# A chunked recurrent scan: key products and their uses in the off-diagonal quarters of the tensor array

## The chip, the cores and the metric

The kernel runs on one core of one Trainium2 chip. The metric is the device time of one execution in microseconds (us). Three runs of the kernel before took 4102.95, 4102.1 and 4114.9 us; the median is 4102.95 us.

## The reference

A two-layer encoder trunk works on two batches, 256 and 1024 tokens of 1024 features, that is 16 heads of 64. Layer 0 mixes tokens with a bidirectional RWKV-7 recurrence, layer 1 with neighbourhood attention, and an MLP follows each. The change is in the recurrence, which is this for every head and direction:

```
def step(S, inp):
    r_t, w_t, k_t, v_t, a_t, b_t = inp
    sa = jnp.einsum('bhvk,bhk->bhv', S, a_t)
    S = S * w_t[:, :, None, :] + sa[..., None] * b_t[:, :, None, :] + v_t[..., None] * k_t[:, :, None, :]
    return S, jnp.einsum('bhvk,bhk->bhv', S, r_t)
```

S is a 64 x 64 state. The backward direction runs the same from the other end, and the two results are added.

## The kernel before, in words

**The stage.** Projections and preparations come first and write to DRAM, per head pair m and direction d, the scaled streams `ar` (columns 0:64 from a, 64:128 from r) and `bk` (columns 0:64 from b, 64:128 from k). Then `scan` (L732) does the recurrence, and the gate, the MLPs and the attention follow. Only `scan` and what it calls is changed.

**Chunks and jobs.** Tokens are taken in chunks of L = 64. Two heads lie on the 128 partitions, head e of the pair on partitions 64e to 64e+63. A job is 16 chunks of one head pair (`scan_job`, L779), in 4 groups g of 4 chunks, for both directions. There are 10 jobs, one after the other, of 16 time steps each; in a step, one chunk of each direction goes through the recurrence. Everything else prepares later steps or finishes earlier ones.

**One pair of matmuls.** `pair` (L967) issues two 64 x 64 matmuls, head 0 on the rows and columns 0 to 63 of the array and head 1 on rows and columns 64 to 127. These are the two diagonal quarters of the array. Operands are fp32.

**Preparation, per group and direction** (so once in two steps): `prod` (L804) makes `aps` = b·(a, r) for 4 chunks, a mask on VectorE turns it into `zb` (L813), `store` sends a part through DRAM for a triangular inverse that VectorE works out in 31 updates per job (`rank1`, L846: a product into `tmp`, L851, and an addition into `q`, L853; "update pair" below), and `merge1` and `merge2` (L895, L903) finish the inverse Q on TensorE (`yps`, `qps`), with copies on ScalarE. `kprod` (L917) makes `kps` = k·(a, r), `kmask` (L924) masks it into `zk` on VectorE, and `ktr` (L928) transposes b and k into `lps`, which ScalarE copies to `lt` (L937). aps, yps, kps, qps and lps, and the transposes `zps` of finished results, share two PSUM buffers in turn (pool `pa`, tag "aps").

**One step of one direction** (`scan_step`, L972), each row a pair of matmuls:

- s0: w = zk(a part)·v. s1: w += a·S, then ScalarE copies w to `up` (L988).
- s1b: yo = zk(r part)·v, yo += r·S; sn = S, sn += k·v.
- s2: us = Q·up, copied to `u` (L1005). s3: sn += b·u, scaled to the next state S (L1011).
- s4: yo += zb·u; VectorE copies or adds yo into y (L1018, L1020).

So a chain w → up → us → u → sn → S → w runs through TensorE and ScalarE for each direction. Each direction has three PSUM banks: `wu` for w and us, `sn`, and `yo`.

**What sets the order.** `at(t, f)` files a piece of work under a time in steps; all pieces are sorted by it and every engine issues its instructions in that order (L765 to L768). An engine that waits at one instruction holds all behind it. Loads go through SyncE's queue (SP) in the same way.

## Time and profile before

| what | value |
| --- | --- |
| median of three runs | 4102.95 us |
| profiled execution, device time | 4111.2 us |
| its span, first to last instruction | 4109.4 us |
| mean granted TensorE clock | 0.969 of full speed |
| TensorE busy in the span | 95% |
| VectorE, ScalarE, GpSimd busy | 56%, 38%, 33% |

In the profile, PE is TensorE's matmuls and PEld its weight loads, DVE is VectorE, ACT is ScalarE, POOL is GpSimd. An fp32 matmul leaves two PE records, one for each of its two passes, so that a pair of matmuls shows as x4. A PE record's duration holds the way through the array, on which the next matmuls already run; what a pair costs is the distance from its start to the start of the next one. "Idle before" is time in which the engine sat idle, with what ended it.

### The profile page before, as it was taken

Reading aid. Unit: us, or ns where it says so; the run is one execution under the profiler, and the core shown is the slowest. Engines: PE = TensorE matmul, PEld = TensorE weight load, DVE = VectorE, ACT = ScalarE, POOL = GpSimd, SP = SyncE. Lnnn points to the kernel's source line nnn. Section 1 sums busy time; section 2 is a strip of 40 time slices with the busy share of each in tenths; the row PEclk is TensorE's granted clock in tenths of the full one; section 3 lists DMA queues with packets and bytes.
Section 4 is the critical chain, followed back from the end, with each engine's and each line's share of the span. In section 5 each row is a group of like instructions: output and inputs, shape, how many; then the busy total and the mean of one; then the engine's idle time right before and its main releaser. Section 6 shows DMA issues by size and latency. Waiting matters only on the chain.

```text
span 4109.4 us, 91128 instructions
## 1 busy us (share of the span) xinstructions
PE 3914.9 (95%) x36820; PEld 3338.7 (81%) x36820; DVE 2290.3 (56%) x4861; ACT 1565.4 (38%) x3788; POOL 1337.8 (33%) x1252
## 2 busy tenths in 40 slices
PE   8989888999999899999999998999989999999999
PEld 5765577898989787888888888887778888888888
DVE  6777743656556457555555563255563755555555
ACT  6776641455555442111111123366563211111111
POOL 4446541112122334222222242244442422222222
PEclk9987888999999999999999999999999999999999
DMA  4226564665554241111111115354455101101101
GB/s 141 71 101 221 207 204 123 154 152 142 135 139 106 82 159 47 42 42 37 36 42 37 36 45 169 101 122 97 111 141 181 46 32 42 42 32 42 42 31 62
DMA packets 429893, 389.65 MB, mean 95 GB/s; under 512 B 246464, under 2 KB 331840, under 8 KB 429472
## 3 DMA queue, kind: packets, MB, share of 16 engines
q1 hardware_dynamic: 395056, 322.48, 27.6%
q10 hardware_dynamic: 34416, 61.35, 4.2%
q8 instruction: 289, 4.73, 0.5%
q14 instruction: 132, 1.08, 0.1%
HBM read 265.26 MB, written 124.44 MB: 95 GB/s over the span
## 4 chain that ended last, share of the span: by engine, by line
PE 80%; DVE 6%; ACT 4%; DMA 4%; issue 2%; POOL 2%; SPq 1%; ACTq 0%; DVEq 0%; POOLq 0%
PE ps L95 18%; PE ps L96 18%; PE ps L97 18%; PE yo L970 2%; PE sn L970 2%; PE wu L970 2%; PE vps L510 2%; PE kps L970 2%; PE lps L970 2%; PE vps L511 1%; PE vps L512 1%; PE aps L970 1%; PE op L1810 1%; DVE q L853 1%; PE pt L1753 1%
## 5 line engine op out<-in xcount | busy, mean ns | idle before, releaser
L1356 DVE TENSOR_TENSOR x<-ps,x 128x256 f32<-128x256 f32 x1488 | 815.2, 596 | 644.9 <-PE ps L97 644.6
L95 PE MATMUL ps<-ah,whi 128*128 128x512 f32 (+1 forms) x2304 | 843.5, 366 | 0.0
L96 PE MATMUL ps<-al,whi 128*128 128x512 f32 (+1 forms) x2304 | 825.7, 358 | 0.4 <-POOL al L1246 0.4
L97 PE MATMUL ps<-ah,wlo 128*128 128x512 f32 (+1 forms) x2304 | 822.6, 357 | 1.8 <-DVE wlo L90 1.5
L90 POOL TENSOR_TENSOR wlo<-raw,whi 128x1024 fp32r<-128x1024 f32 (+1 forms) x178 | 390.3, 2193 | 850.1 <-ACT whi L89 824.3
L95 PE MATMUL ps<-hh,whi 128*128 128x512 f32 (+1 forms) x1536 | 547.9, 357 | 9.5 <-DVE x L1356 9.5
L96 PE MATMUL ps<-hl,whi 128*128 128x512 f32 (+1 forms) x1536 | 546.6, 356 | 0.0
L97 PE MATMUL ps<-hh,wlo 128*128 128x512 f32 (+1 forms) x1536 | 545.9, 355 | 0.0
L95 PEld LDWEIGHTS ps<-ah,whi 128*128 128x128 f32 x2304 | 434.4, 189 | 72.2 <-issue 8.0
L97 PEld LDWEIGHTS ps<-ah,wlo 128*128 128x128 f32 x2304 | 433.4, 188 | 73.0 <-DVE wlo L90 1.9
L96 PEld LDWEIGHTS ps<-al,whi 128*128 128x128 f32 x2304 | 434.6, 189 | 62.8 <-issue 1.0
L89 ACT CAST whi<-raw 128x1024 fp32r<-128x1024 f32 (+1 forms) x206 | 200.4, 973 | 709.4 <-PE ps L96 630.1
L1335 POOL TENSOR_TENSOR rl<-rl 128x512 f32<-128x512 f32 (+1 forms) x192 | 174.0, 906 | 505.9 <-PE ps L97 462.4
L95 PEld LDWEIGHTS ps<-hh,whi 128*128 128x128 f32 x1536 | 291.5, 190 | 54.0 <-DVE x L1356 11.4
L97 PEld LDWEIGHTS ps<-hh,wlo 128*128 128x128 f32 x1536 | 291.7, 190 | 41.8
L96 PEld LDWEIGHTS ps<-hl,whi 128*128 128x128 f32 x1536 | 291.6, 190 | 40.6
L1334 ACT ACTIVATE rl<-ps 128x512 f32<-128x512 f32 (+1 forms) x192 | 100.8, 525 | 555.8 <-PE ps L97 555.8
L1337 ACT CAST hh<-rl 128x512 fp32r<-128x512 f32 (+1 forms) x192 | 105.5, 550 | 323.8 <-POOL rl L1335 323.8
L1338 DVE TENSOR_TENSOR hl<-rl,hh 128x512 fp32r<-128x512 f32 (+1 forms) x192 | 119.8, 624 | 143.2 <-ACT hh L1337 142.6
L1747 POOL TENSOR_TENSOR s<-s,mx 128x384 f32<-128x384 f32 (+1 forms) x150 | 109.8, 745 | 163.4 <-DVE mx L1746 113.6
L1052 POOL TENSOR_TENSOR y<-y,mu 128x512 f32<-128x512 f32 x18 | 20.3, 1125 | 404.6 <-DVE mu L1049 404.6
L1011 ACT ACTIVATE S<-sn,dall 128x64 f32<-128x64 f32 x288 | 90.9, 316 | 156.8 <-PE sn L970 155.0
(301 smaller groups left out, 8262.8 us busy)
## 6 DMA issues: line engine op xcount, KB each, us to landing
raw<-in_w_down_dram SPq DMA_DIRECT2D x64, 512.0 KB
raw<-in_w_up_dram SPq DMA_DIRECT2D x64, 512.0 KB
ar<-ar_d SPq DMA_DIRECT2D x80, 256.0 KB
bk<-bk_d SPq DMA_DIRECT2D x80, 256.0 KB
ar_d<-ar ACTq DMA_DIRECT2D x32, 512.0 KB
bk_d<-bk ACTq DMA_DIRECT2D x32, 512.0 KB
bs<-tab SPq DMA_DIRECT2D x128, 96.0 KB
v_d<-vt ACTq DMA_DIRECT2D x80, 128.0 KB
```

Source lines behind the costliest of these rows:

```text
L89: nc.scalar.copy(hi[:, cs], raw)
L90: lo_eng.tensor_tensor(out=lo[:, cs], in0=raw, in1=hi[:, cs].bitcast(F32), op=ALU.subtract)
L95: mm(ps, sh, mh, start=first, stop=False)
L96: mm(ps, sh, ml, start=False, stop=False)
L97: mm(ps, sl, mh, start=False, stop=last)
L970: self.nc.tensor.matmul(out, w, x, start=kw.get("start", True), stop=kw.get("stop", True))
L1334: nc.scalar.activation(r[:, :n], ps[:, :n], AF.Relu)
L1335: nc.gpsimd.tensor_tensor(out=r[:, :n], in0=r[:, :n], in1=r[:, :n], op=ALU.mult)
L1337: nc.scalar.copy(hh[:, :n], r[:, :n])
L1338: nc.vector.tensor_tensor(out=hl[:, :n], in0=r[:, :n], in1=hh[:, :n].bitcast(F32), op=ALU.subtract)
L1356: nc.vector.tensor_tensor(out=xv, in0=ps[:, :n], in1=xv, op=ALU.add)
L1747: nc.gpsimd.tensor_tensor(out=s[:, :nk], in0=s[:, :nk], in1=mx[:, 2:3].to_broadcast([P, nk]), op=ALU.mult)
```

## The change

`kprod` writes head e's product to the other half of its PSUM tile, partitions of head 1 - e. Its matmul then uses the array's rows of head e and columns of head 1 - e, an off-diagonal quarter. `zk` so has the heads' halves swapped. Its uses, w = zk·v in s0 and yo = zk·v in s1b, read the swapped half and a second copy of v whose halves are swapped too, and write the plain half: these are off-diagonal as well. v is loaded twice for it, into a tile with two planes.

The banks are dealt anew: w has one alone, us lies beside sn in `su`, yo stays. us then starts without clearing its bank, except at the end of a sequence, where no sn precedes it.

The filed times move: s0 from t - 0.22 to t - 0.66, s1b from t + 0.06 to t + 0.01, s4 from t + 0.70 to t + 0.67, and r·S moves from s1b to s4, behind zb·u. The four parts of kprod move from t + 0.80 and on to t - 0.02 and on, so that each stands behind one of the four parts of prod; kmask moves from t + 1.25 to t + 0.60, right behind the mask of aps; kload from t - 1.9 to t - 2.8. bk has 4 buffers instead of 3, zk 5 instead of 3.

```
-        grow(self.r_v, fx, "v", [P, 16, L], 2)
+        grow(self.r_v, fx, "v", [P, 2, 16, L], 2)
...
-  for x, n in (("wu", P), ("sn", L), ("yo", L))] for d in range(2)]
+  for x, n in (("w", L), ("su", P), ("yo", L))] for d in range(2)]
...
-                self.pair(lambda e, z: (ps[z, c, :], bk[z, c, 64:128], ar[z, c, :]))
+                self.pair(lambda e, z: (ps[self.half(1 - e), c, :], bk[z, c, 64:128], ar[z, c, :]))
...
-            at(t - 1.9, kload)
-            at(t + 1.25, kmask)
+            at(t - 2.8, kload)
+            at(t + 0.60, kmask)
             for c in range(4):
-                at(t + c * 0.11 + 0.80, lambda c=c, f=kprod: f(c))
+                at(t + c * 0.133 - 0.02, lambda c=c, f=kprod: f(c))
...
-                for e in range(2):
-                    nc.sync.dma_start(vt[64 * e:64 * e + 64, k:k + n], ...)
+                for i in range(2):
+                    for e in range(2):
+                        nc.sync.dma_start(vt[self.half(e ^ i), i, k:k + n], ...)
...
+    def half(self, e):
+        return slice(64 * e, 64 * e + 64)
...
         def s0():
-            self.pair(lambda e, z: (w()[z], zk[z, c, 0:64], vt[z, cc, :]), stop=new)
+            self.pair(lambda e, z: (w()[z], zk[half(1 - e), c, 0:64], vt[half(1 - e), 1, cc, :]), stop=new)
...
         def s1b():
-            self.pair(lambda e, z: (yo()[z], zk[z, c, 64:128], vt[z, cc, :]), stop=False)
-            if S is not None:
-                self.pair(lambda e, z: (yo()[z], ar[z, c, 64:128], S[z]), start=False, stop=False)
+            self.pair(lambda e, z: (yo()[z], zk[half(1 - e), c, 64:128], vt[half(1 - e), 1, cc, :]), stop=False)
...
         def s2():
-            self.pair(lambda e, z: (us()[z], Q[z, cc, d, :], up[z]))
+            self.pair(lambda e, z: (us()[z], Q[z, cc, d, :], up[z]), start=end, skip=True)
...
         def s4():
-            self.pair(lambda e, z: (yo()[z], zb[z, c, 64:128], u[z]), start=False)
+            self.pair(lambda e, z: (yo()[z], zb[z, c, 64:128], u[z]), start=False, stop=S is None)
+            if S is not None:
+                self.pair(lambda e, z: (yo()[z], ar[z, c, 64:128], S[z]), start=False)
...
-        at(t - 0.22, s0)
+        at(t - 0.66, s0)
         at(t, s1)
-        at(t + 0.06, s1b)
+        at(t + 0.01, s1b)
         at(t + 0.33, s2)
...
-        at(t + 0.70, s4)
+        at(t + 0.67, s4)
```

The order of instructions shows it in two places. The first is on TensorE, where the last transposes of a group (`lps`) end and the next group's aps begins, in the third job; the numbers of the names are buffers, 7206 and 7208 belong to direction 0, 7209 and 7211 to direction 1. Before:

```order
L970 MATMUL lps<-cst,bk 64x64 x4
L970 MATMUL aps<-ar_7174,bb_6166 64x128 [waits DMAHW4_49,DMAHW2_49,PE_49]
L970 MATMUL aps<-ar_7174,bb_6166 64x128
L970 MATMUL wu_7206<-S,ar_7176 64x64 [waits Activation_49]
L970 MATMUL wu_7206<-S,ar_7176 64x64
L970 MATMUL yo_7208<-v_7168,zk 64x64 [waits DVE_49]
L970 MATMUL yo_7208<-v_7168,zk 64x64
L970 MATMUL yo_7208<-S,ar_7176 64x64 x2
```

And now:

```order
L974 MATMUL lps<-cst,bk 64x64 x4
L974 MATMUL aps<-ar_7174,bb_6166 64x128 [waits DMAHW7_49,DMAHW5_49,PE_49]
L974 MATMUL aps<-ar_7174,bb_6166 64x128
L974 MATMUL kps<-ar_7179,bk 64x128 [waits Activation_49]
L974 MATMUL kps<-ar_7179,bk 64x128
L974 MATMUL w_7206<-S,ar_7176 64x64 [waits Activation_49]
L974 MATMUL w_7206<-S,ar_7176 64x64
L974 MATMUL yo_7208<-v_7168,zk 64x64 [waits DVE_49]
```

kps has moved up to stand behind aps. With two buffers in turn, aps takes the one that qps has left and kps the one of the lps just ahead of it, so kps waits for ScalarE's copy of those to lt.

The second place is also on TensorE, where the same group's aps ends and the first half of the inverse's merge (`yps`) begins. Before:

```order
L970 MATMUL aps<-ar_7174,bb_6166 64x128 x2
L970 MATMUL wu_7209<-S,ar_7177 64x64 [waits Activation_49]
L970 MATMUL wu_7209<-S,ar_7177 64x64
L970 MATMUL yps<-qx_7225,zb_7189 64x32 [waits PE_49]
L970 MATMUL yps<-qx_7225,zb_7189 64x32 x7
```

And now:

```order
L974 MATMUL aps<-ar_7174,bb_6166 64x128 x2
L974 MATMUL kps<-ar_7179,bk 64x128 x2
L974 MATMUL w_7209<-S,ar_7177 64x64 [waits Activation_49]
L974 MATMUL w_7209<-S,ar_7177 64x64
L974 MATMUL yo_7211<-v_7168,zk 64x64 [waits DVE_49]
L974 MATMUL yo_7211<-v_7168,zk 64x64
L974 MATMUL su_7210<-S,cst 64x64 x2
L974 MATMUL su_7210<-v_7168,lt 64x64 x2
L974 MATMUL yps<-qx_7225,zb_7189 64x32 [waits DVE_49]
L974 MATMUL yps<-qx_7225,zb_7189 64x32 x7
```

Before, yps waited for no mask, since it took the buffer of the older lps; now both buffers are held, by aps and kps, and it takes the one of aps once VectorE has masked it into zb. Ahead of these rows, between yo<-S of direction 1 and the last aps, now stand another aps and the us of direction 0.

The third place is VectorE's queue around the two masks, in a later job, with the update pairs (tmp, q) and the copies of y. Before:

```order
L1018 COPY y<-yo_7211 128x64 [waits PE_49]
L851 TENSOR_TENSOR tmp<-mt,q 128x231 [waits DVE_49]
L853 TENSOR_TENSOR q<-q,tmp 128x21x11 [waits DVE_49]
L851 TENSOR_TENSOR tmp<-mt,q 128x240 [waits DVE_49]
L853 TENSOR_TENSOR q<-q,tmp 128x20x12 [waits DVE_49]
L813 TENSOR_TENSOR zb_7188<-aps,cst 128x512 [waits DMAHW5_49,PE_49]
L1018 COPY y<-yo_7208 128x64 [waits PE_49]
```

And now:

```order
L1023 COPY y<-yo_7211 128x64 [waits PE_49]
L851 TENSOR_TENSOR tmp<-mt,q 128x231 [waits DVE_49]
L853 TENSOR_TENSOR q<-q,tmp 128x21x11 [waits DVE_49]
L851 TENSOR_TENSOR tmp<-mt,q 128x240 [waits DVE_49]
L853 TENSOR_TENSOR q<-q,tmp 128x20x12 [waits DVE_49]
L813 TENSOR_TENSOR zb_7188<-aps,cst 128x512 [waits PE_49]
L926 TENSOR_TENSOR zk<-kps,cst 128x512 [waits PE_49]
L1023 COPY y<-yo_7208 128x64 [waits PE_49]
```

The mask of kps has moved up to stand behind the mask of aps, ahead of a copy of y. Of the eight masks of aps in a job, three have two update pairs between the copy of y ahead of them and themselves, as here, two have one, and three none.

More of the change, by code (lines that the diff above doesn't have):

```diff
@@ L750, in scan @@
         self.pw = self.sctx.enter_context(tc.tile_pool(name="pw", bufs=1, space=PSUM))
-        self.pbank = [[self.pw.tile([P, n], F32, name=f"{x}{d}") for x, n in (("wu", P), ("sn", L), ("yo", L))] for d in range(2)]
+        self.pbank = [[self.pw.tile([P, n], F32, name=f"{x}{d}") for x, n in (("w", L), ("su", P), ("yo", L))] for d in range(2)]
         self.r_qx, self.r_yt = [[[], 0], [[], 0]], [[[], 0], [[], 0]]
@@ L913, in kload @@
             def kload(d=d, g=g, m=m, c0=c0):
-                bk = J["bk", d, g] = self.rp.tile([P, 4, P], F32, name="bk", tag="bk", bufs=3)
+                bk = J["bk", d, g] = self.rp.tile([P, 4, P], F32, name="bk", tag="bk", bufs=4)
                 nc.sync.dma_start(bk, self.bk_d[m, d, :, c0:c0 + 4, :])
@@ L921, in kprod @@
                 ps = J["pk"]
-                self.pair(lambda e, z: (ps[z, c, :], bk[z, c, 64:128], ar[z, c, :]))
+                self.pair(lambda e, z: (ps[self.half(1 - e), c, :], bk[z, c, 64:128], ar[z, c, :]))
             def kmask(d=d, g=g, ps=None):
-                zk = J["zk"][d, g] = self.rp.tile([P, 4, P], F32, name="zk", tag="zk", bufs=3)
+                zk = J["zk"][d, g] = self.rp.tile([P, 4, P], F32, name="zk", tag="zk", bufs=5)
                 nc.vector.tensor_tensor(out=zk, in0=J["pk"], in1=self.mask[d].unsqueeze(1).to_broadcast([P, 4, P]), op=ALU.mult)
@@ L949, in vload @@
                 rows = slice(c0 * L, (c0 + n) * L)
-                for e in range(2):
-                    nc.sync.dma_start(vt[64 * e:64 * e + 64, k:k + n], vd[rows, m * P + 64 * e:m * P + 64 * e + 64].rearrange("(c s) v -> s c v", s=L))
+                for i in range(2):
+                    for e in range(2):
+                        nc.sync.dma_start(vt[self.half(e ^ i), i, k:k + n], vd[rows, m * P + 64 * e:m * P + 64 * e + 64].rearrange("(c s) v -> s c v", s=L))
         at(-5.423, vload)
@@ L965, in scan_job @@
         self.scan_post(at, J, grp, j == len(self.jobs) - 1)
+    def half(self, e):
+        return slice(64 * e, 64 * e + 64)
     def pair(self, ops, **kw):
         for e in range(2):
-            out, w, x = ops(e, slice(64 * e, 64 * e + 64))
-            self.nc.tensor.matmul(out, w, x, start=kw.get("start", True), stop=kw.get("stop", True))
+            out, w, x = ops(e, self.half(e))
+            self.nc.tensor.matmul(out, w, x, start=kw.get("start", True), stop=kw.get("stop", True), skip_group_check=kw.get("skip", False))
     def scan_step(self, at, t, J, st, d, cc, m, ch, new, end, second):
@@ L975, in scan_step @@
         R = {}
-        w, us, sn, yo = (lambda i=i, s=s: self.pbank[d][i][:, s] for i, s in ((0, slice(0, L)), (0, slice(L, 2 * L)), (1, slice(0, L)), (2, slice(0, L))))
+        w, us, sn, yo = (lambda i=i, s=s: self.pbank[d][i][:, s] for i, s in ((0, slice(0, L)), (1, slice(L, 2 * L)), (1, slice(0, L)), (2, slice(0, L))))
+        half = self.half
         def s0():
             zk, vt = J["zk"][d, g], J["vt"]
-            self.pair(lambda e, z: (w()[z], zk[z, c, 0:64], vt[z, cc, :]), stop=new)
+            self.pair(lambda e, z: (w()[z], zk[half(1 - e), c, 0:64], vt[half(1 - e), 1, cc, :]), stop=new)
         def s1():
-            ar = J["ar"][d, g]
+            ar, zk, vt = J["ar"][d, g], J["zk"][d, g], J["vt"]
             S = R["S"] = None if new else st["S"]
@@ L990, in s1b @@
         def s1b():
-            zk, vt, ar, S = J["zk"][d, g], J["vt"], J["ar"][d, g], R["S"]
-            self.pair(lambda e, z: (yo()[z], zk[z, c, 64:128], vt[z, cc, :]), stop=False)
-            if S is not None:
-                self.pair(lambda e, z: (yo()[z], ar[z, c, 64:128], S[z]), start=False, stop=False)
+            zk, vt, S = J["zk"][d, g], J["vt"], R["S"]
+            self.pair(lambda e, z: (yo()[z], zk[half(1 - e), c, 64:128], vt[half(1 - e), 1, cc, :]), stop=False)
             if not end:
@@ L998, in s1b @@
                     self.pair(lambda e, z: (sn()[z], self.ident[z, z], S[z]), stop=False)
-                self.pair(lambda e, z: (sn()[z], lt[z, c, 1, :], vt[z, cc, :]), start=new, stop=False)
+                self.pair(lambda e, z: (sn()[z], lt[z, c, 1, :], vt[z, 0, cc, :]), start=new, stop=False)
         def s2():
             Q, up = J["Q"], R["up"]
-            self.pair(lambda e, z: (us()[z], Q[z, cc, d, :], up[z]))
+            self.pair(lambda e, z: (us()[z], Q[z, cc, d, :], up[z]), start=end, skip=True)
             u = R["u"] = self.sp.tile([P, L], F32, name="u", tag="u", bufs=4)
@@ L1014, in s4 @@
         def s4():
-            zb, u, y = J["zb"][d, g], R["u"], J["y"]
-            self.pair(lambda e, z: (yo()[z], zb[z, c, 64:128], u[z]), start=False)
+            ar, zb, u, y, S = J["ar"][d, g], J["zb"][d, g], R["u"], J["y"], R["S"]
+            self.pair(lambda e, z: (yo()[z], zb[z, c, 64:128], u[z]), start=False, stop=S is None)
+            if S is not None:
+                self.pair(lambda e, z: (yo()[z], ar[z, c, 64:128], S[z]), start=False)
             if not second:
@@ L1067, in p3a @@
                 for x, m, c0, g in runs:
-                    nc.vector.tensor_tensor(out=st["vb"][:, 4 * x:4 * x + 4], in0=J["vt"][:, 4 * g:4 * g + 4],
+                    nc.vector.tensor_tensor(out=st["vb"][:, 4 * x:4 * x + 4], in0=J["vt"][:, 0, 4 * g:4 * g + 4],
                                             in1=self.bonus[:, c0:c0 + 4, m:m + 1].to_broadcast([P, 4, L]), op=ALU.mult)
```

## The prediction

> **What bounds the kernel now.** I read the page first, then the waits and the groups of the scan's middle, then the timeline of some steps, and last the busy time by stretches of two steps, cut where one group's mask ends and the next begins.

> TensorE is the busiest engine of the page:

> ```profile
> PE 3914.9 (95%) x36820; PEld 3338.7 (81%) x36820; DVE 2290.3 (56%) x4861; ACT 1565.4 (38%) x3788; POOL 1337.8 (33%) x1252
> ```

> An average says little of the scan, so here are eight stretches, which make one job (the fifth of ten): us, then busy us (x count) of PE, PEld, DVE, ACT, POOL, then the clock. Two further rows hold about the last two jobs.

> ```profile
> 1007.62:1016.81 9.19, 9.05 (x272) 8.74 (x268) 8.71 (x25) 4.10 (x16) 1.23 (x1) 1.00 0.34 81
> 1016.81:1026.48 9.67, 9.30 (x272) 8.96 (x268) 8.30 (x22) 5.19 (x20) 4.40 (x6) 1.00 0.67 167
> 1026.48:1033.68 7.20, 6.69 (x201) 6.31 (x196) 5.31 (x15) 2.96 (x13) 2.13 (x3) 1.00 0.43 92
> 1033.68:1042.22 8.54, 8.43 (x260) 8.30 (x258) 7.25 (x24) 4.01 (x17) 0.00 (x0) 1.00 0.48 130
> 1042.22:1050.59 8.37, 8.13 (x240) 7.68 (x236) 3.08 (x13) 5.43 (x18) 0.00 (x0) 1.00 0.41 132
> 1050.59:1059.77 9.18, 9.07 (x278) 8.94 (x276) 3.17 (x10) 4.39 (x18) 0.00 (x0) 1.00 0.66 137
> 1059.77:1067.62 7.85, 7.70 (x236) 7.56 (x233) 3.36 (x11) 3.97 (x15) 3.62 (x5) 1.00 0.77 177
> 1067.62:1078.82 11.20, 8.95 (x227) 8.68 (x224) 4.45 (x20) 6.30 (x21) 3.72 (x4) 0.85 0.75 192
> ```

> ```profile
> 1273.00:1355.00 82.00, 77.65 (x2300) 74.17 (x2298) 46.66 (x141) 44.55 (x169) 20.49 (x25) 1.00 0.42 100
> 1355.00:1420.00 65.00, 55.52 (x1642) 52.42 (x1639) 25.26 (x63) 36.38 (x133) 22.39 (x20) 0.96 0.20 62
> ```

> The job takes 71.2 us, and PE is busy in nearly all of each stretch but the last, where it lacks 2.25 us. So the scan is bound by how fast pairs of matmuls go through the array. VectorE is close behind in stretches 1, 2 and 4 and far behind in the others. The two waits of this part (--waits view of the scan's middle) that matter below:

> ```profile
> PEld lps L970 <- ACT qq L908: 12.2, 49, 0.3
> ACT mt L840 <- DMA mraw<-dd: 10.3, 5, 3.7
> ```

> The second is the gap of the last stretch: a load of the inverse's input holds ScalarE, and with it the chain.

> **What a pair costs.** From the timeline (start, duration):

> ```profile
> 1030.38 0.28 PE L970 MATMUL sn<-u,lt 64*64 64x64 f32 x4
> ...
> 1030.71 0.32 ACT L1011 ACTIVATE S<-sn,dall 128x64 f32<-128x64 f32 x1 [1.13 <-PE sn L970]
> ...
> 1030.85 0.28 PE L970 MATMUL wu<-v,zk 64*64 64x64 f32 x4
> ...
> 1030.97 0.28 PE L970 MATMUL wu<-up,qq 64*64 64x64 f32 x4
> ...
> 1034.64 0.39 PE L970 MATMUL kps<-ar,bk 64*64 64x128 f32 x4
> ...
> 1034.86 0.28 PE L970 MATMUL wu<-up,qq 64*64 64x64 f32 x4
> ```

> wu<-v holds the array 0.12 us (1030.85 to 1030.97), a pair of kps 0.22 us (1034.64 to 1034.86), though their results need 0.28 and 0.39 us to come out. From there to ScalarE is 0.05 us (1030.38 + 0.28 to 1030.71); I take 0.05 us for every such handover, an estimate from this one row.

> **What goes, if the quarters run at once.** Per stretch, 4 pairs of kps (0.88 us), 4 of w = zk·v and 4 of yo = zk·v (8 x 0.12 = 0.96 us) move beside diagonal ones: 1.84 us. Each stands right behind a diagonal pair and ahead of another, which covers it. The start of twelve pairs will not be wholly free; I take 1.7 of 1.84 us, between 0 and 1.84.

> Does the array do that? Nothing here uses four quarters. The nearest rows are in the attention, where the product op of two heads uses all rows and one half of the columns each:

> ```profile
> 2853.30 0.88 PE L1810 MATMUL op<-st,vs 128*64 128x128 f32 x12
> ```

> ```profile
> 2853.30 0.64 PEld L1810 LDWEIGHTS op<-st,vs 128*64 128x64 f32 x12 [0.38 <-DVE mx L1744]
> ```

> These are 12 passes over 128 columns. Two passes side by side took 0.11 us in kps (x4 in 0.22 us, two and two); one by one, at 0.11 us, twelve would take 1.3 us, and they took 0.88 with the way out. So halves of the columns over the same rows do run at once, and the diagonal pairs show that halves of the rows do. Four quarters are the two together, and I think it likely.

> The weight loads of op lie inside the matmuls' time too (0.64 of 0.88 us), over the same rows. [...]

> Also gone is the wait of lps for the copy of qps (12.2 us over about eight jobs, 1.5 us a job): lps now takes the buffer of yps, long copied.

> **What comes, per group.** Durations from the groups of the scan's middle (busy, mean ns):

> ```profile
> L853 DVE TENSOR_TENSOR q<-q,tmp 128x31 f32<-128x31 f32 (+15 forms) x248 | 99.8, 403 | 8.7 <-DVE tmp L851 0.2
> L851 DVE TENSOR_TENSOR tmp<-mt,q 128x31 f32<-128x31 f32 (+15 forms) x248 | 92.6, 373 | 3.5
> L813 DVE TENSOR_TENSOR zb<-aps,cst 128x512 f32<-128x512 f32 x57 | 39.0, 684 | 3.1 <-PE aps L970 3.1
> L937 ACT COPY lt<-lps 128x512 f32<-128x512 f32 x65 | 38.5, 592 | 0.7 <-PE lps L970 0.6
> L1018 DVE COPY y<-yo 128x64 f32<-128x64 f32 x128 | 28.3, 221 | 29.1 <-PE yo L970 26.8
> ```

> First, kps waits for lt. From the start of the last lps pair: 0.28 out + 0.05 + 0.59 copy + 0.05 = 0.97 us. TensorE has that pair (0.12) and one of aps (0.22) to do meanwhile. It stands for 0.63 us, and behind it the whole queue: w<-S of direction 0, yo, sn.

> Second, yps waits for the mask zb, and VectorE reaches it behind the copy of y and the update pairs (0.40 + 0.37 = 0.78 us each). From the start of yo<-S: 0.28 + 0.05 + 0.22 + n x 0.78 + 0.68 + 0.05 = 1.28 + 0.78 n. TensorE has seven pairs before yps (yo, aps, us, aps, w, and sn twice), two of them of aps: 5 x 0.12 + 2 x 0.22 = 1.04 us. It stands 1.02 us for n = 1 and 1.80 us for n = 2. For n = 0 the mask starts when aps has come out: 0.39 + 0.05 + 0.68 + 0.05 = 1.17 us from its last pair, less 0.22 + 3 x 0.12 of work, 0.59 us. Three, two and three groups of a job: 3 x 0.59 + 2 x 1.02 + 3 x 1.80 = 9.2 us. Behind yps stands sn<-u, the end of the chain of direction 0, so nothing goes on.

> Third, with fewer pairs between them, the links of the chain can show. From sn<-u to w<-S after yps: 0.28 + 0.05 + 0.32 + 0.05 = 0.70 us, with four to five pairs between (0.5 to 0.6): 0 to 0.15 us a stretch, 0.6 us a job.

> **What costs nothing.** The shared bank of us and sn: between their writes stand the copies that the chain waits for anyway, and s0, now filed 0.44 of a step earlier, has its bank alone and waits for nothing; in the old bank it would stand behind the copy of u, some 0.2 us. Two more loads of v a job, and kload moved ahead on SP past the loads of ar and bb: DMA engines are at 0.34 to 0.77 in the stretches, and v is asked for over five steps ahead; if that cover went, a load would hold a job's start, 0 to 4 us in all. The mask zk ahead of a copy of y delays that by 0.68 us, while TensorE is in yps and the chain; if that does not fit, it is the third rival.

> **The sum.** Jobs 0 to 7, each: -8 x 1.7 - 1.5 + 8 x 0.63 + 9.2 + 0.6 = -0.3 us. The gain is eaten by the two new waits, 14.2 us a job; for eight jobs about 0. The last two jobs have no aps left (it belongs to jobs further on), so kps and yps find their buffers free. There the gain stays, less what the chain allows: 8 x 1.7 = 13.6 at most, a few us at least; I take 10 each. In all -20 us. Against the profiled execution, 4111.2 us, that is 4091; against the median, 4102.95, on which I forecast, **4083 us**. About 0.3% (12 us) is what a measurement here can tell from no change.

> **The rivals.**

> 1. *The new waits are covered.* If TensorE finds VectorE and ScalarE ahead of it, both waits shrink, and the stretches end at their floors: PE less 1.7, or DVE where that is more (9.0, 8.6, 5.5, 7.5 in the first four with some idle between instructions, then 6.4, 7.4, 6.0, 9.5): 60 against 71, 11 us a job, 88 for eight, with the last two 108 us. That is 3995 in full and 4049 with half of it; I say 4015. For it: DVE is idle a good half of the last four stretches. Against it: both waits come from the order, not from load. Chance 0.22.
> 2. *Slower: the quarters take turns.* If an off-diagonal pair starts only when the diagonal one is through, the 13.6 us a job do not go, and both waits come all the same; yps loses a kps and a yo pair of waiting (0.34 x 8 = 2.7). +13.3 - 2.7 = +10.6 a job, 85 for eight, none in the last two: 4188. It decides at the share of 1.7 us that is really covered: the last two jobs and the -0.3 us of the others bear 22 us, so with 0.3 us a stretch uncovered in 80 stretches, that is at 1.4, the gain is gone. For it: no row shows four quarters. Against: op. [...] Chance 0.17.
> 3. *VectorE's copies of y become the wait.* yo<-v waits for a copy of y four times a stretch; with zk ahead of it and fewer pairs between, 0.1 to 0.2 us each, 26 to 51 us in eight jobs: 4109 to 4134. The row of L1018 shows DVE waiting for PE, not PE for DVE, which speaks against. Chance 0.16.

> The forecast keeps 0.45. Its own range is 4060 to 4110: 1.84 or 1.5 us covered is -9 or +13 us over 64 stretches, the chain 0 to 1.2 a job -5 or +5, the last two jobs 13 or 5 each -6 or +10.

> **Range and chances.** 4000 to 4160 leaves out most of the second rival and the lower end of the first. Faster by over 0.3% (below 4091): the first rival and about 0.65 of the forecast's, 0.51. Within 0.3%: 0.13 of the forecast and 0.05 of the third, 0.18. Slower: 0.03 + 0.11 + 0.17 = 0.31.

> **What would show it.** Right: rows of kps in which a pair starts with its neighbour of aps, so that the two take 0.22 us together; idle time of PE before kps, ended by ACT lt, near 0.6 us, 64 times; before yps, ended by DVE zb, 0.6 to 1.8 us, 62 times; jobs 0 to 7 still near 70 us and the last two about 10 us shorter each. Wrong: PE stretches as long as before in busy time (the second rival), little idle time before kps and yps (the first), or idle time before yo, ended by DVE y (the third).

## The result, and the profile after

The changed kernel is slower: 4146.11 us (median; 4144.45 to 4159.35) beside 4102.89 us of the kernel before on the same chip, ratio 1.0105, 95% interval 1.0078 to 1.0133. The forecast was 4083 us. The profiled executions are 4144.8 us (span 4143.0) and 4111.2 us (span 4109.4). In the rows of after the line numbers of scan_step are 3 to 5 higher than before (its products L974, y L1023, u L1008, S L1014).

TensorE's line on the page after:

```profile
PE 3831.2 (92%) x36820; PEld 3226.9 (78%) x36820; DVE 2287.0 (55%) x4861; ACT 1559.4 (38%) x3788; POOL 1337.6 (32%) x1252
```

TensorE is busy 84 us less (3914.9 before), and the span is 33.6 us longer. Where that is, the busy time by stretches tells: first jobs 0 to 7 of before, then its last two jobs (us, then busy us and count of PE, PEld, DVE, ACT, POOL, then TensorE's granted clock).

```profile
731.30:1291.10 559.80, 528.99 (x15108) 509.93 (x15108) 345.90 (x1015) 287.64 (x1057) 112.97 (x135) 0.98 0.58 141
...
1291.10:1412.20 121.10, 115.33 (x3422) 109.77 (x3420) 57.02 (x174) 65.15 (x255) 28.25 (x31) 1.00 0.30 84
```

The same of after:

```profile
741.00:1336.60 595.60, 466.02 (x15132) 424.47 (x15134) 346.68 (x1016) 284.58 (x1057) 112.89 (x135) 0.94 0.57 138
...
1336.60:1447.10 110.50, 98.07 (x3418) 89.26 (x3410) 56.72 (x172) 62.51 (x255) 28.36 (x31) 0.98 0.33 92
```

Three pieces make the 33.6 us: the first step starts 9.7 us later (731.3, 741.0), jobs 0 to 7 take 35.8 us more, the last two jobs 10.6 us less, and 1.3 us go in what follows. In jobs 0 to 7 TensorE's busy time fell by 63 us, its idle time rose from 30.8 (559.8 - 529.0) to 129.6 us (595.6 - 466.0), and its granted clock fell from 0.98 to 0.94.

The waits of TensorE in jobs 0 to 7 after (from 741 to 1334 us; each row: us in all, times, longest):

```profile
PE yps L974 <- DVE zb L813: 65.4, 62, 1.8
PE kps L974 <- ACT lt L937: 35.7, 62, 1.1
PE yo L974 <- ACT u L1008: 7.1, 7, 1.0
...
PE yo L974 <- DVE y L1023: 3.1, 12, 0.4
```

Both new waits are there, 62 times each, that of yps up to the 1.8 us that was forecast. One of them, in the timeline of after, with a piece of four quarters at work ahead of it:

```profile
963.93 0.28 PE L974 MATMUL kps<-ar,bk 64*64 64x128 f32 x2
...
963.97 0.28 PE L974 MATMUL aps<-ar,bb 64*64 64x128 f32 x2
...
964.04 0.28 PE L974 MATMUL kps<-ar,bk 64*64 64x128 f32 x2
...
964.09 0.28 PE L974 MATMUL aps<-ar,bb 64*64 64x128 f32 x2
...
964.15 0.22 PE L974 MATMUL w<-v,zk 64*64 64x64 f32 x2
...
964.26 0.28 PE L974 MATMUL kps<-ar,bk 64*64 64x128 f32 x2
...
965.41 0.68 DVE L813 TENSOR_TENSOR zb<-aps,cst 128x512 f32<-128x512 f32 x1
...
966.15 0.66 PE L974 MATMUL yps<-qx,zb 64*64 64x32 f32 x16 [1.31 <-DVE zb L813]
```

Each of these rows of kps and aps is half a pair. The halves of kps start 0.11 us apart (963.93, 964.04), as before, and those of aps between them (963.97, 964.09): two pairs go through in the 0.22 us that a kps pair alone took before. A few pairs later TensorE stands 1.31 us, until the mask on VectorE is through.

What nothing in the prediction had: the clock. A stretch of another job of after with several waits in it, and what follows it:

```profile
1034.00:1037.50 3.50, 1.81 (x50) 1.36 (x50) 1.75 (x5) 2.76 (x8) 2.55 (x3) 1.00 0.72 200
1037.50:1039.50 2.00, 2.00 (x60) 1.87 (x52) 1.07 (x5) 0.33 (x2) 0.00 (x0) 0.54 0.77 202
1039.50:1042.00 2.50, 1.79 (x35) 1.57 (x32) 1.45 (x4) 0.58 (x2) 0.00 (x0) 0.50 0.88 185
1042.00:1046.00 4.00, 3.99 (x116) 3.96 (x116) 3.67 (x14) 1.72 (x7) 0.06 (x1) 0.69 0.65 160
```

TensorE is busy 1.81 of 3.50 us; then it runs at half its clock for about 7 us (in them a yps takes 1.07 us, at 1040.27, where the one above took 0.66). Over jobs 0 to 7 a clock of 0.94 means 36 us lost if TensorE is busy in those stretches (0.06 x 595.6; here it is, in 7.78 of 8.50 us), against 11 us before (0.02 x 559.8): some 25 us, an estimate from these rows. No single stand in these jobs is longer than 1.8 us. The trace's record of the clock has fifteen half-clock stretches that begin in jobs 0 to 7 of after, each of 3.4 or 6.8 us, and in the 3.4 us ahead of each TensorE was busy only 38 to 61%. That is no sharp bound: nine other stretches of 3.4 us with TensorE busy 50 to 61% were not followed by half clock. So the clock was halved here after short stands (busy 1.81 of 3.50 us in the rows above), without a long one; what sets the moment is not shown by any view here. The first half-clock stretch of job 0 is another thing, which the start left behind:

```profile
741.00:750.90 9.90, 9.52 (x196) 9.14 (x198) 6.28 (x22) 4.18 (x14) 0.00 (x0) 0.50 0.53 140
```

The clock was half already from 713.4 us on, with TensorE busy 10.59 of the 27.60 us up to 741.0. The kernel before began its job 0 at a clock of 1.00. So some 5 of the 25 us (half of 9.90) look like the price of the waits for loads ahead of the first step (experiment 6), and not of the two new waits.

### The profile page after: what moved, and what is told of

The parts are those of the page before. It is cut to its first block, busy times and chain, and to the rows that moved or that the text cites. A ratio compares the mean times of both kernels' runs of the same rounds, so it can differ in the third digit from the quotient of the medians.

```text
span 4143.0 us, 91157 instructions
## 1 busy us (share of the span) xinstructions
PE 3831.2 (92%) x36820; PEld 3226.9 (78%) x36820; DVE 2287.0 (55%) x4861; ACT 1559.4 (38%) x3788; POOL 1337.6 (32%) x1252
## 4 chain that ended last, share of the span: by engine, by line
PE 76%; DVE 9%; ACT 6%; DMA 4%; issue 3%; POOL 2%; SPq 1%; ACTq 0%; DVEq 0%; POOLq 0%
PE ps L95 18%; PE ps L96 18%; PE ps L97 18%; PE su L974 2%; PE yo L974 2%; PE vps L510 1%; DVE q L853 1%; PE vps L511 1%; PE vps L512 1%; DVE tmp L851 1%; PE yps L974 1%; PE op L1815 1%; DVE zb L813 1%; PE lps L974 1%; PE pt L1758 1%
## 5 line engine op out<-in xcount | busy, mean ns | idle before, releaser
L974 PE MATMUL kps<-ar,bk 64*64 64x128 f32 x1280 | 126.6, 294 | 35.9 <-ACT lt L937 35.7
```

What stands on the lines that cost most here:

```text
L974: self.nc.tensor.matmul(out, w, x, start=kw.get("start", True), stop=kw.get("stop", True), skip_group_check=kw.get("skip", False))
```

## The experiments

The theory (A): the four quarters do run at once, and the gain is eaten by the two waits for PSUM buffers, by the halved clock that they bring, and by the start. The rival (B) differs by run. Each time stands beside runs of the kernel before on the same chip; ratios are to that kernel, with 95% intervals.

**1. Diagonal again.** kps, w<-v and yo<-v back on the diagonal quarters, in the order of after:

```diff
-                self.pair(lambda e, z: (ps[self.half(1 - e), c, :], bk[z, c, 64:128], ar[z, c, :]))
+                self.pair(lambda e, z: (ps[z, c, :], bk[z, c, 64:128], ar[z, c, :]))
...
-            self.pair(lambda e, z: (w()[z], zk[half(1 - e), c, 0:64], vt[half(1 - e), 1, cc, :]), stop=new)
+            self.pair(lambda e, z: (w()[z], zk[z, c, 0:64], vt[z, 0, cc, :]), stop=new)
...
-            self.pair(lambda e, z: (yo()[z], zk[half(1 - e), c, 64:128], vt[half(1 - e), 1, cc, :]), stop=False)
+            self.pair(lambda e, z: (yo()[z], zk[z, c, 64:128], vt[z, 0, cc, :]), stop=False)
```

> The changed kernel with kps, w<-v and yo<-v put back on the diagonal quarters, everything else (order, buffers, loads) as changed. Theory A, the four quarters do run at once and the time went to the new waits, to TensorE's clock in them and to the start: TensorE gets back some 11 us of busy time a job, of which up to 4 us a job lie in what are now waits, so 4146 + 7 to 11 us x 10 = 4215 to 4255 us. Theory B, off-diagonal pairs give little and the longer jobs are the price of the quarters themselves: 4135 to 4160 us.

Measured: 4178.3 us, ratio 1.0173 (1.0152 to 1.0194). Its jobs 0 to 7, and its two waits:

```profile
743.50:1364.40 620.90, 544.14 (x15124) 507.57 (x15126) 348.70 (x1012) 288.20 (x1057) 112.87 (x135) 1.00 0.55 133
```

```profile
PE kps L974 <- ACT lt L937: 33.6, 63, 1.0
PE yps L974 <- DVE zb L813: 24.8, 40, 1.2
```

Both theories missed the time, which lies between them. But the busy time settles the quarters: 544.1 us at full clock beside 466.0 us with 36 lost, so some 114 us in eight jobs (1.78 us a stretch; I had taken 1.7 of 1.84). The clocks are read to two places, which leaves 3 us or so either way. Only 25 of these reach the end (595.6 beside 620.9 us), for two reasons: a TensorE with more to do comes later to yps and waits 24.8 instead of 65.4 us, so that its idle time in all is 77 instead of 130 us, and its clock, with TensorE busy 88% of the time instead of 78%, is 1.00 instead of 0.94. What the quarters give, the waits and the clock take.

**2 and 3. The waits away.** First yps alone is filed later, then kps too:

```diff
-            at(t + 0.52, merge1)
+            at(t + 0.90, merge1)
```

> The changed kernel with one number changed: yps is filed 0.38 of a step later, so that the mask zb has that much longer. Theory A: the idle time of TensorE before yps (62.5 us over the middle of the scan) goes, and with it some of the half-clock time that follows it: 4146 - 50 to 85 = 4060 to 4095 us. Theory B, the waits only take up slack of a chain that is late anyway: the idle time comes back ahead of w<-S or sn<-u, and the time stays within 20 us, 4126 to 4150 us.

```diff
-                at(t + c * 0.133 - 0.02, lambda c=c, f=kprod: f(c))
+                at(t + c * 0.133 + 0.13, lambda c=c, f=kprod: f(c))
```

> The same, and kps filed 0.15 of a step later too, so that the copy lt is through before it. Theory A: both waits go (62.5 and 33.3 us of TensorE's idle time) and half-clock time falls from 322 us towards the 259 us of the kernel before, some 25 us more: 4146 - 85 to 120 = 4026 to 4061 us, clearly faster than the kernel before. Theory B: 4126 to 4150 us, the idle time turning up ahead of the chain's links.

Measured: 4114.04 us, ratio 1.0013 (1.0001 to 1.0025), then 4102.96 us, ratio 0.9990 (0.9976 to 1.0003). Both times lie between A and B. So the two waits cost about 1.15% of the time, 47 us (1.0105 against 0.9990), far more than B allowed and half of what A said. What is left in the second version, jobs 0 to 7:

```profile
732.90:1281.80 548.90, 458.20 (x15120) 422.40 (x15120) 337.49 (x1016) 280.19 (x1058) 112.88 (x135) 0.95 0.63 150
```

```profile
PE yps L974 <- DVE zb L813: 17.9, 27, 1.5
PE zps L974 <- DVE zb L813: 17.1, 14, 1.5
PE yo L974 <- DVE y L1023: 8.1, 18, 0.7
...
PE su L974 <- issue: 5.0, 7, 1.3
PE aps L974 <- issue: 4.1, 3, 2.3
```

The wait for kps is gone, that for yps is 18 instead of 65 us, and zps, the transposition of finished rows, now stands behind the mask in its place. The clock did not come back (0.95), where A had counted on 25 us: the two waits are not all that halves it. And there is a new kind of stand, "issue", in which TensorE waits for nothing that the profile shows.

**4. The key products at their old times**, on their new quarters:

```diff
-            at(t - 2.8, kload)
-            at(t + 0.60, kmask)
+            at(t - 1.9, kload)
+            at(t + 1.25, kmask)
...
-                at(t + c * 0.133 - 0.02, lambda c=c, f=kprod: f(c))
+                at(t + c * 0.11 + 0.80, lambda c=c, f=kprod: f(c))
```

> The changed kernel with the key products (their load, products and mask) filed at their old times, but on their off-diagonal quarters, and w, su, yo as changed. Theory A: the order of the PSUM buffers is the old one, so neither kps waits for lt nor yps for zb, lps waits for the copy of qps again (1.5 us a job), and the quarters still overlap with whatever pair stands beside them: 4146 - 60 to 110 = 4036 to 4086 us. Theory B: no gain over the kernel before beyond its own uncertainty, 4095 to 4150 us.

Measured: 4094.55 us, ratio 0.9974 (0.9962 to 0.9987), just at the lower edge of B and 8 us above A. Jobs 0 to 7:

```profile
744.40:1288.20 543.80, 473.46 (x15108) 442.13 (x15108) 342.20 (x1016) 280.55 (x1057) 112.90 (x135) 0.96 0.64 151
```

16 us less than the kernel before and 52 less than after, with the same array work: the order in which the key products were filed carries the loss.

**5. The halved clock.** Work that nothing needs is put where TensorE stands. First small pairs of 64 columns, 5 ahead of each yps and 4 ahead of each kps (x8), then, after that run, one wide pair at each of these places (x11, shown), for jobs 0 to 7:

```diff
+                self.fill(d, 320 if j < 8 else 0)
                 yps = self.pt.tile([P, 4, 32], F32, name="yps", tag="aps")
...
+                    self.fill(d, 256 if j < 8 else 0)
                     J["pk"] = self.pa.tile([P, 4, P], F32, name="kps", tag="aps")
...
+    def fill(self, d, n):
+        if n:
+            self.pair(lambda e, z: (self.pbank[d][1][z, P:P + n], self.ident[z, z], self.cst[z, 0:n]), start=False, skip=True)
```

> The changed kernel with work added that nothing needs: 5 more pairs (ident by ident, into spare columns of su's bank) ahead of each yps and 4 ahead of each kps of jobs 0 to 7, some 0.5 us each where TensorE now stands for 1.06 and 0.57 us on average. Theory A, the halved clock behind the waits is a good part of the loss: with TensorE kept busy the half-clock stretches in the steps of jobs 0 to 7 (73 us of them) mostly go, and the time falls although there is more to do: 4121 to 4141 us. Theory B, the halved clock costs next to nothing, the waits alone count: 4144 to 4165 us.

> The changed kernel with one unneeded pair of 320 columns ahead of each yps and one of 256 ahead of each kps of jobs 0 to 7 (some 0.55 and 0.45 us where TensorE stands 1.06 and 0.57), in 4 records each where the version with many small pairs had 20 and 16. Theory A, the half clock behind the waits costs some 27 us in jobs 0 to 7, and the small pairs lost their gain to their number: 4121 to 4141 us, with half-clock time in the steps near 30 us. Theory B, the halved clock costs little in itself because TensorE catches up before the next wait: 4144 to 4160 us.

Measured: 4159.09 us, ratio 1.0122 (1.0094 to 1.0150), as B of x8 had it; then 4132.29 us, ratio 1.0059 (1.0041 to 1.0078), as A of x11 had it. Jobs 0 to 7 of x11, and its waits up to 1376 us:

```profile
742.20:1322.80 580.60, 504.99 (x15628) 420.94 (x15628) 348.68 (x1014) 282.30 (x1057) 112.89 (x135) 0.99 0.60 142
```

```profile
PE yps L982 <- DVE zb L815: 31.3, 45, 1.3
PE su L982 <- ACT u L1016: 14.3, 40, 0.6
```

With 128 unneeded pairs TensorE is 39 us longer busy, its clock is back at 0.99, and the jobs take 15 us less than in after. So the stands cost more than their length: keeping TensorE busy in them is worth at least those 15 us, and what came back with it is the clock. By the estimate above its whole price is 25. In the whole time the two kernels' intervals, 1.0078 to 1.0133 and 1.0041 to 1.0078, just touch. In x8 the clock came back too (0.98), but the many small pairs gave the gain away:

```profile
742.30:1341.00 598.70, 517.94 (x17352) 478.30 (x17352) 346.85 (x1016) 283.02 (x1058) 112.68 (x135) 0.98 0.58 138
```

**6. The start.** The first two jobs take in four head pairs each, so with the second plane of v there are 16 loads of it for each of them instead of 8. On SP's queue they stand ahead of the loads of Q and qx. Their issue for job 0, before and after:

```profile
704.89 5.21 SPq L951 DMA_DIRECT2D v<-v_d  x8
```

```profile
708.78 10.48 SPq L952 DMA_DIRECT2D v<-v_d  x16
```

That is 5.3 us more for SP before it comes to Q. TensorE's waits before the first step, before and after:

```profile
PE aps L970 <- DMA ar<-ar_d: 8.8, 1, 8.8
PE yps L970 <- DMA qx<-qd: 6.8, 1, 6.8
...
PE aps L970 <- DMA bb<-bk_d: 1.9, 2, 1.4
```

```profile
PE yps L974 <- DMA qx<-qd: 12.8, 1, 12.8
PE aps L974 <- DMA ar<-ar_d: 8.3, 1, 8.3
PE aps L974 <- DMA bb<-bk_d: 3.9, 1, 3.9
```

Of the 9.7 us 4.4 are not the change's: the last vps behind a copy vt starts at 650.75 before and at 655.12 us after, ahead of all that is touched, and in other versions at 647.5 to 659.0 us. From there to the first step it is 80.6 us before (to 731.34) and 85.9 after (to 741.02): 5.3 us, as much as the eight issues take. Three other places were tried: behind Q (in after, and with the old times of the key products), behind Q, ar and bb (the same with -3.2), and on ScalarE's queue:

```diff
-        at(-5.423, vload)
+        at(-5.423, lambda: vload((0,) if j < 2 else (0, 1)))
+        if j < 2:
+            at(-4.6, lambda: vload((1,)))
```

```diff
-                        nc.sync.dma_start(vt[self.half(e ^ i), i, k:k + n], vd[rows, m * P + 64 * e:m * P + 64 * e + 64].rearrange("(c s) v -> s c v", s=L))
+                        (nc.scalar if i and j < 2 else nc.sync).dma_start(vt[self.half(e ^ i), i, k:k + n], vd[rows, m * P + 64 * e:m * P + 64 * e + 64].rearrange("(c s) v -> s c v", s=L))
```

> The changed kernel; for jobs 0 and 1 the loads of v's second, swapped plane are filed behind the loads of Q and qx on SP's queue instead of ahead of them. Theory A, the eight added loads ahead of Q held the first step: the gap of TensorE before the first yps falls from 12.8 us back towards 6.8 us, the first step comes 5 to 8 us earlier, 4138 to 4141 us. Theory B, SP has room and the first step is late for another reason (the masks' or the updates' place): the gap stays above 11 us, 4143 to 4149 us.

> The changed kernel with the key products at their old times (4094.6 us measured) and the second plane's loads of jobs 0 and 1 behind Q. Theory A, the two costs are independent: 5 to 8 us less, 4086 to 4090 us, 0.4 to 0.6% below the kernel before. Theory B, the start's gap isn't SP's: 4092 to 4097 us.

> The changed kernel with the key products at their old times (4094.6 us measured), and the second plane's loads of v for jobs 0 and 1 filed 2.2 steps later, behind the loads of Q, qx, ar and bb. Theory A, the start was held by these loads' place on SP: neither the gap before the first yps nor that before aps is above 8 us, together 8 to 10 us where it was 16.3, and the time is 4085 to 4090 us. Theory B, whatever stands behind them on SP is late instead: 4092 to 4097 us, as when they stood behind Q alone.

> The changed kernel with the key products at their old times (4094.6 us measured), and the second plane's loads of v for jobs 0 and 1 issued from ScalarE's queue, which stands idle there for some 25 us, instead of SP's. Theory A, SP's queue is full at the start, so that eight more loads cost 5.3 us wherever they stand on it, and nothing on another queue: from the first matmul behind the last vt copy to the first step it is again some 80.5 us, as in the kernel before, and not 85 to 86, and the time is 4087 to 4092 us. Theory B, the DMA engines or the memory hold the loads of Q, not the queue: still 84 us or more, and 4092 to 4097 us.

Measured: 4148.62 us, ratio 1.0093 (1.0063 to 1.0123); 4094.44 us, ratio 0.9965 (0.9952 to 0.9979); 4093.87 us, ratio 0.9962 (0.9948 to 0.9976); 4091.29 us, ratio 0.9961 (0.9946 to 0.9976). The first is B in the time, and shows how: the wait of yps falls to 7.5 us as A said, and that of aps for bb rises from 3.9 to 7.6 us, because the loads of v now stand ahead of bb's.

```profile
PE yps L976 <- DMA qx<-qd: 7.8, 2, 7.5
PE aps L976 <- DMA bb<-bk_d: 7.6, 1, 7.6
```

Behind Q, ar and bb, yps waits 7.9 us and aps 2.3 for bb, but aps then waits 5.5 us for the copy qq. From the last vps to the first step it is 86.1 us with the old times alone, 85.1 with the plane behind Q and 84.6 with it behind all three.

On ScalarE's queue it is 82.7 us from the last vps (657.20) to the first step (739.89), 3.2 less than in after; both waits are near those of before, but TensorE waits 10.9 instead of 8.3 us for the load of ar:

```profile
PE aps L974 <- DMA ar<-ar_d: 10.9, 1, 10.9
PE yps L974 <- DMA qx<-qd: 7.7, 1, 7.7
```

In all four versions with the second plane off the place ahead of Q, yps waits 7.5 to 8.5 us instead of 12.8, so that wait goes with SP's queue. How much of the 5.3 us is the queue's stays open. Each version was profiled once, and the versions that leave these loads in their place stand at 83.5 to 87.7 us (x11 and x8), of which 82.7 is clear by 0.8 only. That the DMA engines hold the rest was not tried. In the whole time these last versions can't be told apart from x7, by their intervals.

**7. What is late next.** The version with both waits away, without most of VectorE's work, then with fewer instructions for TensorE. Both leave out what the result needs (most updates of the inverse, then most transposes too) and serve for their times alone:

```diff
-            at(T3, rank1, 1 if j == 0 else 3)
+            if jj == 31:
+                at(T3, rank1, 1 if j == 0 else 3)
```

> The version with yps and kps both filed later (4103.0 us measured), and of the inverse's 31 update pairs a job only the first is kept, so that Q is not the inverse; all else is issued as before. It leaves some 22 us of VectorE's work out of each job. Theory A, with the two waits gone the next thing late is VectorE, whose in-order queue puts masks, copies of y and the sums of the norm behind update pairs: jobs 2 to 7 fall from 69.7 to about 60 us, the floor of TensorE and the chain, 4103 - 50 to 80 = 4023 to 4053 us. Theory B, TensorE's own work, the handovers and the round trip of the inverse's input at the end of each job set the pace: 4083 to 4103 us.

```diff
-                for i in range(2):
-                    self.pair(lambda e, z: (ps[z, c, i, :], bk[z, c, 64 * i:64 * i + 64], self.ident[z, z]))
+                if c == 0:
+                    self.pair(lambda e, z: (ps[z].rearrange("p c i l -> p (c i) l"), bk[z, c, 0:64], self.ident[z, z].unsqueeze(1).to_broadcast([64, 8, 64])))
```

> The version without update pairs (4073.7 us measured, 66 us a job), and the eight pairs of lps of a group are one pair over eight copies of ident: as many columns, 4 records of TensorE where 32 were, and lt holds copies of one transposed block. Theory A, that version is held by the supply of TensorE's instructions (it stands 0.3 to 1.6 us with no wait, each time a multiple of 254 records after the last, 4.3 us a block): 224 of 3872 records a job less are 3.8 us a job, 4036 to 4050 us. Theory B, these stands are something else and the array's columns or the chain set the pace: 4066 to 4078 us.

Measured: 4073.72 us, ratio 0.9915 (0.9889 to 0.9940), and 4041.09 us, ratio 0.9843 (0.9825 to 0.9861). The first lies between A and B, 20 us above A: with VectorE half empty and the clock at 0.99, TensorE is idle for 79 us of eight jobs, 52 of them as "issue":

```profile
743.00:1263.20 520.20, 441.43 (x15120) 406.82 (x15120) 179.15 (x534) 280.59 (x1058) 109.28 (x135) 0.99 0.66 158
```

```profile
PE yo L975 <- issue: 13.3, 15, 1.6
PE su L975 <- issue: 11.1, 17, 1.4
PE lps L975 <- issue: 9.5, 13, 1.4
```

Counted through the records of PE and PEld, each of these 70 stands comes a multiple of 254 records (to within four) after the one before. The row of the instruction queue in the --dma view of the same window:

```profile
q8 instruction: 118, 1.93, 1.6%
```

118 packets of 16.4 KB in 520 us, one every 4.41 us. At 254 records a packet, the 30240 records make 119; that the packets hold TensorE's instructions is read from these two counts alone. The kernel before fetched as many in 559.8 us, one every 4.74 us, and stood in this way three times, 1.2 us in all. The second run bears this out: it sends as many columns through the array (443 us busy) in 12% fewer records (some 440 a job; the expectation had counted half of them), the stands as "issue" fall from 52 to 21 us, the packets from 118 to 105, and the jobs from 520 to 498 us.

```profile
739.70:1237.50 497.80, 443.11 (x13324) 365.31 (x13328) 176.87 (x534) 276.04 (x1057) 109.34 (x135) 0.97 0.70 166
```

That is theory A of that run, in the time too. How a packet comes to be late is not shown by any view here.

**8. Fewer records, for the same result.** In x12's version sn<-S, a pair with two quarters of ident, is made one matmul with all of it:

```diff
-                    self.pair(lambda e, z: (sn()[z], self.ident[z, z], S[z]), stop=False)
+                    nc.tensor.matmul(sn(), self.ident, S, start=True, stop=False)
```

> The same as the version with the old times and the later loads of v, and sn<-S is one matmul of the whole ident over 128 rows instead of a diagonal pair (the same sum). Theory A, fewer records help where the supply is short, 60 of 3870 a job, up to 1 us: 2 to 8 us less than that version. Theory B, a matmul that takes all four quarters cannot run beside an off-diagonal pair, and stops both ways of the array ahead of it: 5 to 25 us more.

Measured: 4119.98 us, ratio 1.0036 (1.0022 to 1.0050), 26 us more than without it: theory B. TensorE's busy time in eight jobs, the version without it first:

```profile
736.90:1278.40 541.50, 468.35 (x15110) 437.12 (x15108) 344.07 (x1016) 281.04 (x1058) 112.83 (x135) 0.97 0.64 152
```

```profile
741.50:1298.60 557.10, 526.69 (x14710) 477.28 (x14708) 344.90 (x1015) 283.32 (x1057) 113.07 (x135) 0.99 0.62 148
```

58 us more, at a higher clock at that, for the 200 matmuls that took the place of pairs (400 rows of TensorE fewer, two a matmul): some 0.29 us more each. The jobs take 16 us more. The busy time shows the price of such a matmul; that it is the way through all four quarters which stops its neighbours, as B said, was not tried by itself. In this version TensorE is idle for 30 us of the eight jobs (557.1 - 526.7), without the new matmul for 73 (541.5 - 468.4).

## Why the prediction was wrong

The sign was wrong, and the forecast was 63 us short. The sum for jobs 0 to 7, term by term, in us for eight jobs:

| term | forecast | measured | from |
|---|---|---|---|
| quarters, 8 x 1.7 a job | -109 | -114 | diagonal again against after, at full clock |
| waits (kps, yps, chain, less lps's) | +107 | +125 | idle time +99, and 26 in TensorE's busy time |
| TensorE's clock | not in the sum | +25 | 0.98 to 0.94 |
| together | -2 | +36 | 559.8 to 595.6 |

- *The quarters run at once*: right, to within 5%. The second rival is refuted: kps and aps load weights for the same rows and go through together, two pairs in the 0.22 us of one (963.93 to 964.15, where the next pair, w<-v, starts).
- *The two waits*: right in place, number and cause. kps stood 0.58 us (35.7 / 62) where 0.63 was said, yps 1.05 us (65.4 / 62) where 1.15 was the mean. But the term as a whole was 18 us too small. 26 us lie beside the idle time: on the diagonal in the order of after, TensorE is busy 544 us, where before it was 529 less 11 for the clock. This looks like the way out of the last pair, 0.28 less 0.12 us, which counts as busy at each stand (16 us for the 63 and 40 of that run); that was not tried by itself.
- *The step that failed* is the sum itself: -13.6 + 14.2 was taken as even, with the clock of TensorE as given. The rows for it were quoted: the stretch in which TensorE lacked 2.25 us had a clock of 0.85, all others 1.00. A change that puts 16 stands in each job, and takes a fifth of TensorE's work out, had to be asked what the clock would do. It cost some 25 us, the greatest part of the 38 us by which these jobs were missed; the wide pairs bear out at least 15. The two waits are not its only cause: 5 us of it are the start's, and in the versions without most of the waits (x4, x7) the clock is 0.95 and 0.96. What keeps it low there stays open.
- *What costs nothing* failed as well: the loads of v, costed at 0 to 4 us and hidden, go with 5.3 us at the start. "Two more loads of v a job" is wrong for the first two jobs, which have eight more each, and "DMA engines at 0.34 to 0.77" spoke of the engines in the steady state and not of SP's queue at the start, where eight more issues (10.48 instead of 5.21 us) stand ahead of the load that TensorE waits for.
- *The last two jobs*: -10.6 where -20 was said. TensorE is 17 us less busy there, where the quarters could give 27, and it is idle 12.4 instead of 5.8 us, at a clock of 0.98 instead of 1.00.
- *The first rival* (waits covered) came true only where the order was changed, and even then not its 4015 us: 4091 to 4094, as other things come next: in the version with the old times (x7), waits for the copies of y (14.0 us) and for S (12.2), stands as "issue" (17) and the clock (0.96). *The third* is small: 3.1 us of waits for y.

Forecast and measured then differ by 38 us in jobs 0 to 7, 9.4 in the last two and 9.7 at the start, 4.4 of which lie ahead of all that was changed. The rest of the 63 us is how the profiled executions stand to their medians, before 8.3 above and after 1.3 below, less 1.3 behind the scan and 2 of rounding in the forecast's sum.

Best of the versions that leave nothing out are those with the key products at their old times on their new quarters, 0.26 to 0.39% below the kernel before (the latter with the second plane's loads on ScalarE's queue).

## What to carry to other kernels

Work taken off the bounding engine is a gain only as far as the order gives it something else to do: where a product is moved, list which reader of the shared PSUM ring it will now stand behind, and price that beside the work saved. On TensorE price the stands twice, once for their length (here 99 us more idle time) and once for the clock (here some 20 us, an estimate: the 25 above less 5 for the start), and read both off the stretches of the profile before. And count instructions as well as columns: with the waits and most of VectorE's work away, 52 of the 79 us that TensorE stood had no wait to be seen (x10), which looks like the supply of its instructions.
